# Rotary embedding: fp16 input resident from eight early loads, sums on TensorE, fp32 stores from SyncE

## Chip, cores and metric

The kernel runs on one core of one Trainium2 chip. The metric is the device time of one execution in microseconds, as the median over runs; lower is better.

## What is computed

The reference applies a rotary position embedding, with scaled positions, to x of shape 8 x 8 x 1024 x 64 (batch, heads, sequence, head size) in fp32. `scale` is 0.5.

```python
half = x.shape[-1] // 2
angles = np.outer(positions * scale, freqs)          # 1024 x 32
cos, sin = np.cos(angles), np.sin(angles)
out_first  = x[..., :half] * cos - x[..., half:] * sin
out_second = x[..., :half] * sin + x[..., half:] * cos
out = concatenate([out_first, out_second], axis=-1)  # fp32
```

The input and the output are 16.8 MB each. The cosine and sine depend on the position and the frequency, not on batch or head.

## The kernel before

The 64 (batch, head) pairs are taken as 16 units of four. In a unit, a partition holds 16 positions of a head: 64 partitions make one head, the 128 partitions hold two heads, and the free dimension holds two such pairs (`PU = 2`), 2 x 1024 elements. In DRAM each of these rows of 1024 elements is 4 KB of fp32.

Unit 0 is loaded as fp32 by SyncE (line 71). The positions (line 76, two transfers) and the frequencies (line 81) follow on the same queue. Units 1 to 15 are loaded by GpSimd's queue (line 90) with a cast to fp16 on the way, into seven rotating buffers; five are issued ahead of the loop, and each pass of the loop issues one more. GpSimd's queue also carries every store (line 153), which casts the fp16 result to fp32 on the way out, so loads and stores run through one queue in the order of issue.

The setup makes the tables: TensorE spreads the scaled frequencies over the partitions (line 86), VectorE forms the angles in turns (lines 97 to 116), 128 x 512, and ScalarE takes the sine four times (line 120), so that the table of the cosine and that of the sine each hold their 32 values twice in a row, for both halves of a head. They are fp16.

For each unit VectorE does four instructions: `pc`, the unit times the cosine (line 138), `ps`, the unit times the sine (line 139), each 128 x 2048, and the two half-width sums, a difference for the first halves (line 144) and a sum for the second (line 148), each 128 x 1024. The tile framework puts in the waits and orders the instructions of an engine by priority: in the trace the product `pc` of the next unit often stands ahead of the sums of the one before.

Of the kernel before, what the change touches and what calls it, by code (L numbers as in the profile page):

```python
# [1 line left out]

# [1 line left out]

# [4 lines left out]

FP32 = mybir.dt.float32
FP16 = mybir.dt.float16
AF = mybir.ActivationFunctionType
ALU = mybir.AluOpType

_MAGIC = 12582912.0
_TWO_PI_DN = float(np.float32(np.uint32(0x40C90FDA).view(np.float32)))

PAIRS_PER_UNIT = 2
PREFETCH = 5  # L20
BUF_X = 7
BUF_O = 7
BUF_P = 3


@with_exitstack
def kernel(
    ctx: ExitStack,
    tc: tile.TileContext,
    x: bass.AP,  # L30
    freqs: bass.AP,
    positions: bass.AP,
    scale: bass.AP,
    out: bass.AP,
):
    nc = tc.nc

    B, Hh, S, D = x.shape
    NBH = B * Hh
    half = D // 2  # L40
    P = nc.NUM_PARTITIONS
    HP = P // 2
    K = S // HP
    KD = K * D
    PU = PAIRS_PER_UNIT
    NU = NBH // (2 * PU)
    UKD = PU * KD
    assert S % HP == 0 and D == 2 * half and NBH % (2 * PU) == 0

    fscale = float(scale)  # L50

    xv = x.rearrange("b h s d -> (b h) (s d)")
    ov = out.rearrange("b h s d -> (b h) (s d)")

    def unit_dram(t, u):
        return t.rearrange("(i r) n -> i (r n)", r=2)[
            u * PU : (u + 1) * PU, :
        ].rearrange("i (p n) -> p i n", n=KD)

    consts = ctx.enter_context(tc.tile_pool(name="consts", bufs=1))  # L60
    tmp = ctx.enter_context(tc.tile_pool(name="tmp", bufs=2))
    psum = ctx.enter_context(tc.tile_pool(name="psum", bufs=1, space=bass.MemoryType.PSUM))
    xin0 = ctx.enter_context(tc.tile_pool(name="xin0", bufs=1))
    xin = ctx.enter_context(tc.tile_pool(name="xin", bufs=BUF_X))
    xout = ctx.enter_context(tc.tile_pool(name="xout", bufs=BUF_O))
    prods = ctx.enter_context(tc.tile_pool(name="prods", bufs=BUF_P))

    xtiles: dict[int, bass.AP] = {}

    X0 = xin0.tile([P, PU, KD], FP32)  # L70
    nc.sync.dma_start(out=X0, in_=unit_dram(xv, 0))  # L71
    xtiles[0] = X0

    pos_i64 = consts.tile([P, K], positions.dtype)
    for u in (0, 1):
        nc.sync.dma_start(  # L76
            out=pos_i64[u * HP : (u + 1) * HP, :],
            in_=positions.rearrange("(q k) -> q k", k=K),
        )
    freq_row = consts.tile([1, half], FP32)  # L80
    nc.sync.dma_start(out=freq_row, in_=freqs[None, :])

    coef = consts.tile([1, P], FP32)
    nc.vector.memset(coef, fscale / (2.0 * np.pi))  # L84
    cfreq = psum.tile([P, half], FP32)
    nc.tensor.matmul(out=cfreq, lhsT=coef, rhs=freq_row, start=True, stop=True)  # L86

    def load_unit(u):
        X = xin.tile([P, PU, KD], FP16, tag="X")
        nc.gpsimd.dma_start(out=X, in_=unit_dram(xv, u))  # L90
        xtiles[u] = X

    for u in range(1, min(1 + PREFETCH, NU)):
        load_unit(u)

    posf = consts.tile([P, K], FP32)
    nc.vector.tensor_copy(  # L97
        out=posf,
        in_=pos_i64.bitcast(mybir.dt.int32).rearrange("p (k t) -> p k t", t=2)[:, :, 0],
    )  # L100
    y = tmp.tile([P, K, half], FP32)
    nc.vector.tensor_tensor(  # L102
        out=y,
        in0=posf.unsqueeze(2).broadcast_to((P, K, half)),
        in1=cfreq.unsqueeze(1).broadcast_to((P, K, half)),
        op=ALU.mult,
    )
    yc = tmp.tile([P, K, half], FP32)
    nc.vector.tensor_scalar(out=yc, in0=y, scalar1=0.25, scalar2=None, op0=ALU.add)  # L109

    tabs = consts.tile([P, 2, K, D], FP16)
    for i, src in enumerate((yc, y)):
        m = tmp.tile([P, K, half], FP32, tag="m")
        nc.vector.tensor_scalar(out=m, in0=src, scalar1=_MAGIC, scalar2=None, op0=ALU.add)  # L114
        rneg = tmp.tile([P, K, half], FP32, tag="rneg")
        nc.vector.scalar_tensor_tensor(  # L116
            out=rneg, in0=m, scalar=_MAGIC, in1=src, op0=ALU.subtract, op1=ALU.subtract
        )
        for h in (0, 1):
            nc.scalar.activation(  # L120
                out=tabs[:, i, :, h * half : (h + 1) * half],
                in_=rneg,
                func=AF.Sin,
                bias=0.0,
                scale=-_TWO_PI_DN,
            )
    cosT = tabs[:, 0, :, :].rearrange("p k d -> p (k d)").unsqueeze(1).broadcast_to((P, PU, KD))
    sinT = tabs[:, 1, :, :].rearrange("p k d -> p (k d)").unsqueeze(1).broadcast_to((P, PU, KD))

    for u in range(NU):  # L130
        if u + 1 + PREFETCH < NU:
            load_unit(u + 1 + PREFETCH)
        X = xtiles.pop(u)
        OUT = xout.tile([P, PU, KD], FP16, tag="O")

        pc = prods.tile([P, PU, KD], FP16, tag="pc")
        ps = prods.tile([P, PU, KD], FP16, tag="ps")
        nc.vector.tensor_tensor(out=pc, in0=X, in1=cosT, op=ALU.mult)  # L138
        nc.vector.tensor_tensor(out=ps, in0=X, in1=sinT, op=ALU.mult)  # L139

        pcv = pc.rearrange("p i (k d) -> p (i k) d", d=D)
        psv = ps.rearrange("p i (k d) -> p (i k) d", d=D)
        ov_ = OUT.rearrange("p i (k d) -> p (i k) d", d=D)
        nc.vector.tensor_tensor(  # L144
            out=ov_[:, :, 0:half], in0=pcv[:, :, 0:half], in1=psv[:, :, half:D],
            op=ALU.subtract,
        )
        nc.vector.tensor_tensor(  # L148
            out=ov_[:, :, half:D], in0=psv[:, :, 0:half], in1=pcv[:, :, half:D],
            op=ALU.add,  # L150
        )

        nc.gpsimd.dma_start(out=unit_dram(ov, u), in_=OUT)  # L153


# [1 line left out]
_INS = ['x', 'freqs', 'positions', 'scale']  # L157
_OUTS = [((8, 8, 1024, 64), 'float32')]
#: Inputs that are plain numbers.
_NUMBERS = {'scale': 0.5}  # L160


# [26 lines left out]
```

## Time and profile before

| | |
|---|---|
| median of 4 runs | 87.27 us (86.94 to 87.54) |
| the profiled execution | 87.23 us |
| its span, first to last instruction | 85.3 us |
| VectorE busy | 61.4 us, 72 instructions |
| ScalarE busy | 3.5 us, 5 instructions |
| TensorE busy | 0.6 us, 2 instructions |
| GpSimd busy (it includes issuing transfers) | 22.6 us, 35 instructions |
| bytes read from and written to DRAM | 16.79 MB and 16.78 MB |
| transfers on GpSimd's queue | 8432 packets, 24.64 MB |
| transfers on SyncE's queue | 434 packets, 1.07 MB |

Busy times are sums over instructions that may overlap a little at their ends. Packet bytes are counted where they land, so a load that casts to fp16 counts half of what it reads. The difference of 1.93 us between the profiled execution and its span lies before the first and after the last instruction.

### The profile page before, as it was taken

How to read it: one execution, taken by the hardware profiler on the slowest of the kernel's cores; microseconds unless marked ns; L12 is line 12 of the kernel's file. 1: busy time of each engine (PE TensorE's matmuls, PEld its weight loads, DVE VectorE, ACT ScalarE, POOL GpSimd, SP SyncE). 2: the span in 40 equal slices, each digit the busy share in tenths (PEclk: the TensorE clock that was granted, in tenths of full speed). 3: DMA queues.
4: the chain of work that ended last, by engine and by line, in shares of the span. 5: the costliest groups of instructions: out<-in, count | busy, mean ns of one | idle time of the engine just before them, and what ended most of it. 6: DMA issues, size and time to landing. Idle time of an engine off the chain costs nothing.

```text
span 85.3 us, 193 instructions
## 1 busy us (share of the span) xinstructions
PE 0.6 (1%) x2; PEld 0.5 (1%) x2; DVE 61.4 (72%) x72; ACT 3.5 (4%) x5; POOL 22.6 (26%) x35
## 2 busy tenths in 40 slices
PE   0001000000000000000000000000000000000000
PEld 0001000000000000000000000000000000000000
DVE  0000879999999999999999999999998992000000
ACT  6000063000000000000000000000000000000000
POOL 4990000005215162460633612303213033000000
DMA  1899999999999999999999999999999999999970
GB/s 13 321 286 214 210 209 215 210 209 210 307 357 224 429 376 284 321 348 244 419 221 394 272 322 350 255 410 215 394 279 327 423 421 426 424 432 421 426 240 0
DMA packets 8867, 25.72 MB, mean 301 GB/s; under 512 B 674, under 2 KB 674, under 8 KB 8866
## 3 DMA queue, kind: packets, MB, share of 16 engines
q0 software_dynamic: 8432, 24.64, 107.3%
q1 hardware_dynamic: 434, 1.07, 3.7%
q14 instruction: 1, 0.01, 0.0%
HBM read 16.79 MB, written 16.78 MB: 394 GB/s over the span
## 4 chain that ended last, share of the span: by engine, by line
DVE 31%; DMA 22%; issue 20%; POOL 6%; SPq 2%; ACT 1%; POOLq 1%; PE 1%
DMA X<-in_x_dram 15%; DVE pc L138 11%; DVE ps L139 9%; DMA freq_row<-in_freqs_dram 6%; POOL out_dram L153 6%; DVE OUT L148 4%; DVE OUT L144 4%; ACT tabs L120 1%; SPq L76 1%; DVE m L114 1%; POOLq L184 1%; DVE y L102 1%; PE cfreq L86 1%; DVE rneg L116 1%; SPq L71 1%
## 5 line engine op out<-in xcount | busy, mean ns | idle before, releaser
L153 POOL DMA_DIRECT2D out_dram<-OUT x16 | 11.5, 720 | 47.8 <-DVE OUT L148 45.7
L138 DVE TENSOR_TENSOR pc<-X,tabs 128x2048 f16<-128x2048 f16 (+1 forms) x16 | 20.6, 1287 | 0.8 <-ACT tabs L120 0.6
L139 DVE TENSOR_TENSOR ps<-X,tabs 128x2048 f16<-128x2048 f16 (+1 forms) x16 | 20.6, 1287 | 0.0
L90 POOL DMA_DIRECT2D X<-in_x_dram x15 | 10.9, 727 | 1.2 <-POOLq L170 0.8
L144 DVE TENSOR_TENSOR OUT<-pc,ps 128x1024 f16<-128x1024 f16 x16 | 11.0, 687 | 0.0
L148 DVE TENSOR_TENSOR OUT<-ps,pc 128x1024 f16<-128x1024 f16 x16 | 11.0, 685 | 0.0
L97 DVE CAST posf<-pos_i 128x16 f32<-128x16 int32 x1 | 0.2, 175 | 7.1 <-DMA pos_i<-in_positions_dram 7.1
L120 ACT ACTIVATE tabs<-rneg 128x512 f16<-128x512 f32 x4 | 2.2, 618 | 9.3 <-DVE rneg L116 9.3
L120 ACT ACT_TABLE_LOAD x1 | 1.3, 1283 | 0.7 <-PEq L170 0.7
L102 DVE TENSOR_TENSOR y<-posf,cfreq 128x512 f32<-128x512 f32 x1 | 0.7, 689 | 0.6 <-PE cfreq L86 0.6
L84 DVE MEMSET coef<- 1x128 f32 x1 | 0.2, 165 | 0.8 <-PEq L170 0.8
L116 DVE SCALAR_TENSOR_TENSOR rneg<-m,y 128x512 f32<-128x512 f32 x1 | 0.7, 685 | 0.0
L116 DVE SCALAR_TENSOR_TENSOR rneg<-m,yc 128x512 f32<-128x512 f32 x1 | 0.7, 684 | 0.0
L86 PE MATMUL cfreq<-freq_row,coef 1*128 1x32 f32 x2 | 0.6, 391 | 8.1 <-DMA freq_row<-in_freqs_dram 8.1
L86 PEld LDWEIGHTS cfreq<-freq_row,coef 1*128 1x128 f32 x2 | 0.5, 308 | 8.1 <-issue 8.1
L109 DVE TENSOR_SCALAR yc<-y 128x512 f32<-128x512 f32 x1 | 0.4, 428 | 0.0
L114 DVE TENSOR_SCALAR m<-yc 128x512 f32<-128x512 f32 x1 | 0.4, 426 | 0.0
L114 DVE TENSOR_SCALAR m<-y 128x512 f32<-128x512 f32 x1 | 0.4, 419 | 0.0
L170 POOL MEMSET const-float32-0.0<- 128x1 f32 x1 | 0.1, 93 | 0.3 <-issue 0.3
L170 POOL MEMSET const-bfloat16-1.0<- 128x1 bf16 x1 | 0.1, 96 | 0.0
L170 POOL MEMSET const-float32-1.0<- 128x1 f32 x1 | 0.1, 93 | 0.0
L170 POOL MEMSET const-uint8-127<- 128x1 uint8 x1 | 0.1, 93 | 0.0
## 6 DMA issues: line engine op xcount, KB each, us to landing
out_dram<-OUT POOLq DMA_DIRECT2D x16, 1024.0 KB, 12.5
X<-in_x_dram POOLq DMA_DIRECT2D x15, 512.0 KB, 12.1
X<-in_x_dram SPq DMA_DIRECT2D x1, 1024.0 KB, 4.9
pos_i<-in_positions_dram SPq DMA_DIRECT2D x2, 8.0 KB, 5.3
freq_row<-in_freqs_dram SPq DMA_DIRECT2D x1, 0.1 KB
```

What stands on the lines that cost most here:

```text
L71: nc.sync.dma_start(out=X0, in_=unit_dram(xv, 0))
L86: nc.tensor.matmul(out=cfreq, lhsT=coef, rhs=freq_row, start=True, stop=True)
L90: nc.gpsimd.dma_start(out=X, in_=unit_dram(xv, u))
L102: nc.vector.tensor_tensor(out=y, in0=posf.unsqueeze(2).broadcast_to((P, K, half)), in1=cfreq.unsqueeze(1).broadcast_to((P, K, half)), op=A ...
L114: nc.vector.tensor_scalar(out=m, in0=src, scalar1=_MAGIC, scalar2=None, op0=ALU.add)
L116: nc.vector.scalar_tensor_tensor(out=rneg, in0=m, scalar=_MAGIC, in1=src, op0=ALU.subtract, op1=ALU.subtract)
L120: nc.scalar.activation(out=tabs[:, i, :, h * half : (h + 1) * half], in_=rneg, func=AF.Sin, bias=0.0, scale=-_TWO_PI_DN,)
L138: nc.vector.tensor_tensor(out=pc, in0=X, in1=cosT, op=ALU.mult)
L139: nc.vector.tensor_tensor(out=ps, in0=X, in1=sinT, op=ALU.mult)
L144: nc.vector.tensor_tensor(out=ov_[:, :, 0:half], in0=pcv[:, :, 0:half], in1=psv[:, :, half:D], op=ALU.subtract,)
L148: nc.vector.tensor_tensor(out=ov_[:, :, half:D], in0=psv[:, :, 0:half], in1=pcv[:, :, half:D], op=ALU.add,)
L153: nc.gpsimd.dma_start(out=unit_dram(ov, u), in_=OUT)
```

## The change

The layout, the queues and the place of the sums change.

- A unit is still four heads, but a partition holds 32 positions of one head: 32 partitions a head, one row of 2048 elements (8 KB of fp32) a partition. The position and angle tiles are therefore twice as wide, 128 x 1024 for the angles.
- All of x is resident: unit 0 as fp32 from SyncE, units 1 to 15 as fp16 by seven loads of 1, 1, 2, 2, 3, 3 and 3 units from GpSimd's queue, all issued ahead of the loop. No load waits for a buffer.
- Positions (four transfers) and frequencies are issued from ScalarE's queue.
- The cosine table holds its 32 values once and is read with a zero step for the two halves. The sine table holds minus sine for the first half and sine for the second.
- The two sums leave VectorE. GpSimd builds an fp16 identity; TensorE multiplies it with `pc` and then with `ps`, whose halves are read in swapped order, accumulating in PSUM: four pairs of 512-column matmuls a unit. The sign in the sine table turns the sum into the difference where it is wanted.
- ScalarE copies each 128 x 1024 of PSUM (two banks; three such buffers) to an fp32 output tile of 128 x 2048; there are six of these.
- SyncE stores the output tile without a cast.

```diff
-PAIRS_PER_UNIT = 2
-PREFETCH = 5
-BUF_X = 7
-BUF_O = 7
+GROUPS = (1, 1, 2, 2, 3, 3, 3)
+BUF_O = 6
 BUF_P = 3
+BANK = 512
...
-    HP = P // 2
+    HEADS = 4
+    HP = P // HEADS
     K = S // HP
-    KD = K * D
+    N = K * D
...
-    X0 = xin0.tile([P, PU, KD], FP32)
-    nc.sync.dma_start(out=X0, in_=unit_dram(xv, 0))
+    X0 = xin.tile([P, N], FP32, name="X0")
+    nc.sync.dma_start(out=X0, in_=xv[:, 0, :])
...
-    for u in (0, 1):
-        nc.sync.dma_start(
+    for h in range(HEADS):
+        nc.scalar.dma_start(
...
-    nc.sync.dma_start(out=freq_row, in_=freqs[None, :])
+    nc.scalar.dma_start(out=freq_row, in_=freqs[None, :])
+
+    u0 = 1
+    for g, n in enumerate(GROUPS):
+        X = xin.tile([P, n, N], FP16, name=f"X{g + 1}")
+        nc.gpsimd.dma_start(out=X, in_=xv[:, u0 : u0 + n, :])
+        for i in range(n):
+            xtiles[u0 + i] = X[:, i, :]
+        u0 += n
+
+    ident = consts.tile([P, P], FP16)
+    nc.gpsimd.memset(ident, 0.0)
+    nc.gpsimd.affine_select(
+        out=ident, in_=ident, compare_op=ALU.not_equal, fill=1.0, base=0,
+        pattern=[[-1, P]], channel_multiplier=1,
+    )
...
+    cosT = consts.tile([P, K, half], FP16)
+    sinT = consts.tile([P, K, 2, half], FP16)
...
+    nc.scalar.activation(out=cosT, in_=rc, func=AF.Sin, bias=0.0, scale=-_TWO_PI_DN)
+    rs = reduced(y, "s")
+    for h, sign in ((0, -1.0), (1, 1.0)):
+        nc.scalar.activation(
+            out=sinT[:, :, h, :], in_=rs, func=AF.Sin, bias=0.0, scale=sign * _TWO_PI_DN
+        )
+    cos_b = cosT.unsqueeze(2).broadcast_to((P, K, 2, half))
...
-        nc.vector.tensor_tensor(
-            out=ov_[:, :, 0:half], in0=pcv[:, :, 0:half], in1=psv[:, :, half:D],
-            op=ALU.subtract,
-        )
-        nc.vector.tensor_tensor(
-            out=ov_[:, :, half:D], in0=psv[:, :, 0:half], in1=pcv[:, :, half:D],
-            op=ALU.add,
-        )
-
-        nc.gpsimd.dma_start(out=unit_dram(ov, u), in_=OUT)
+        OUT = xout.tile([P, N], FP32, tag="O")
+        for b in range(N // BLK):
+            acc = psum.tile([P, KB, 2, half], FP32, tag="acc")
+            for c in range(BLK // BANK):
+                kk = BANK // D
+                kl = slice(c * kk, (c + 1) * kk)
+                kg = slice(b * KB + c * kk, b * KB + (c + 1) * kk)
+                nc.tensor.matmul(out=acc[:, kl, :, :], lhsT=ident, rhs=pc[:, kg, :, :], start=True, stop=False)
+                nc.tensor.matmul(out=acc[:, kl, :, :], lhsT=ident, rhs=ps[:, kg, ::-1, :], start=False, stop=True)
+            nc.scalar.copy(
+                out=OUT[:, b * BLK : (b + 1) * BLK], in_=acc.rearrange("p k h j -> p (k h j)")
+            )
+        nc.sync.dma_start(out=ov[:, u, :], in_=OUT)
```

The helper `reduced` holds the two VectorE instructions that before stood in the table loop (add and subtract a large constant, to take off whole turns); the multiplications `pc` and `ps` keep their form, with `cos_b` and `sinT` as tables.

More of the change, by code (lines that the diff above doesn't have):

```diff
@@ L12 @@
 FP16 = mybir.dt.float16
+I32 = mybir.dt.int32
 AF = mybir.ActivationFunctionType
@@ L41 @@
     P = nc.NUM_PARTITIONS
-    HP = P // 2
+    HEADS = 4
+    HP = P // HEADS
     K = S // HP
-    KD = K * D
[L45 to L48, printed above, removed]
-    fscale = float(scale)
[L52 to L58, printed above, removed]
+    N = K * D
+    NU = NBH // HEADS
+    BLK = 2 * BANK
+    KB = BLK // D
+    assert S % HP == 0 and D == 2 * half and NBH % HEADS == 0 and sum(GROUPS) == NU - 1
+    fscale = float(scale)
+    xv = x.rearrange("b h s d -> (b h s d)").rearrange("(u p n) -> p u n", p=P, n=N)
+    ov = out.rearrange("b h s d -> (b h s d)").rearrange("(u p n) -> p u n", p=P, n=N)
     consts = ctx.enter_context(tc.tile_pool(name="consts", bufs=1))
[L61 to L64, printed above, removed]
+    tmp = ctx.enter_context(tc.tile_pool(name="tmp", bufs=1))
+    setup_psum = ctx.enter_context(tc.tile_pool(name="setup_psum", bufs=1, space=bass.MemoryType.PSUM))
+    psum = ctx.enter_context(tc.tile_pool(name="psum", bufs=3, space=bass.MemoryType.PSUM))
+    xin = ctx.enter_context(tc.tile_pool(name="xin", bufs=1))
     xout = ctx.enter_context(tc.tile_pool(name="xout", bufs=BUF_O))
     prods = ctx.enter_context(tc.tile_pool(name="prods", bufs=BUF_P))
-    xtiles: dict[int, bass.AP] = {}
-    X0 = xin0.tile([P, PU, KD], FP32)
-    nc.sync.dma_start(out=X0, in_=unit_dram(xv, 0))
-    xtiles[0] = X0
+    X0 = xin.tile([P, N], FP32, name="X0")
+    nc.sync.dma_start(out=X0, in_=xv[:, 0, :])
+    xtiles = {0: X0}
     pos_i64 = consts.tile([P, K], positions.dtype)
-    for u in (0, 1):
-        nc.sync.dma_start(
-            out=pos_i64[u * HP : (u + 1) * HP, :],
+    for h in range(HEADS):
+        nc.scalar.dma_start(
+            out=pos_i64[h * HP : (h + 1) * HP, :],
             in_=positions.rearrange("(q k) -> q k", k=K),
@@ L80 @@
     freq_row = consts.tile([1, half], FP32)
-    nc.sync.dma_start(out=freq_row, in_=freqs[None, :])
+    nc.scalar.dma_start(out=freq_row, in_=freqs[None, :])
[12 more added lines that the diff above has]
+    )
     coef = consts.tile([1, P], FP32)
     nc.vector.memset(coef, fscale / (2.0 * np.pi))
-    cfreq = psum.tile([P, half], FP32)
+    cfreq = setup_psum.tile([P, half], FP32)
     nc.tensor.matmul(out=cfreq, lhsT=coef, rhs=freq_row, start=True, stop=True)
[L88 to L94, printed above, removed]
     posf = consts.tile([P, K], FP32)
@@ L98 @@
         out=posf,
-        in_=pos_i64.bitcast(mybir.dt.int32).rearrange("p (k t) -> p k t", t=2)[:, :, 0],
+        in_=pos_i64.bitcast(I32).rearrange("p (k t) -> p k t", t=2)[:, :, 0],
     )
@@ L107, with reduced @@
     )
[L108 to L113, printed above, removed]
+    cosT = consts.tile([P, K, half], FP16)
+    sinT = consts.tile([P, K, 2, half], FP16)
+    def reduced(src, tag):
+        m = tmp.tile([P, K, half], FP32, name="m" + tag)
         nc.vector.tensor_scalar(out=m, in0=src, scalar1=_MAGIC, scalar2=None, op0=ALU.add)
-        rneg = tmp.tile([P, K, half], FP32, tag="rneg")
+        rneg = tmp.tile([P, K, half], FP32, name="rneg" + tag)
         nc.vector.scalar_tensor_tensor(
@@ L118 @@
         )
[L119 to L125, printed above, removed]
-            )
[L127 to L144, printed above, removed]
-            out=ov_[:, :, 0:half], in0=pcv[:, :, 0:half], in1=psv[:, :, half:D],
-            op=ALU.subtract,
-        )
-        nc.vector.tensor_tensor(
-            out=ov_[:, :, half:D], in0=psv[:, :, 0:half], in1=pcv[:, :, half:D],
-            op=ALU.add,
-        )
-        nc.gpsimd.dma_start(out=unit_dram(ov, u), in_=OUT)
@@ new lines, in reduced @@
+        return rneg
+    yc = tmp.tile([P, K, half], FP32)
+    nc.vector.tensor_scalar(out=yc, in0=y, scalar1=0.25, scalar2=None, op0=ALU.add)
+    rc = reduced(yc, "c")
+    nc.scalar.activation(out=cosT, in_=rc, func=AF.Sin, bias=0.0, scale=-_TWO_PI_DN)
[5 more added lines that the diff above has]
+    cos_b = cosT.unsqueeze(2).broadcast_to((P, K, 2, half))
@@ new lines @@
+    for u in range(NU):
+        X = xtiles.pop(u).rearrange("p (k h j) -> p k h j", h=2, j=half)
+        pc = prods.tile([P, K, 2, half], FP16, tag="pc")
+        ps = prods.tile([P, K, 2, half], FP16, tag="ps")
+        nc.vector.tensor_tensor(out=pc, in0=X, in1=cos_b, op=ALU.mult)
+        nc.vector.tensor_tensor(out=ps, in0=X, in1=sinT, op=ALU.mult)
+        OUT = xout.tile([P, N], FP32, tag="O")
[9 more added lines that the diff above has]
+                out=OUT[:, b * BLK : (b + 1) * BLK], in_=acc.rearrange("p k h j -> p (k h j)")
+            )
+        nc.sync.dma_start(out=ov[:, u, :], in_=OUT)
```

## The prediction

> **What bounds the kernel now.** I read the page's slices first, then the stages by windows, then the groups, then the waits. Slices (section 2 of the page; each digit is the busy tenth of one fortieth of the span, 2.13 us):
>
> ```profile
> DVE  0000879999999999999999999999998992000000
> DMA  1899999999999999999999999999999999999970
> GB/s 13 321 286 214 210 209 215 210 209 210 307 357 224 429 376 284 321 348 244 419 221 394 272 322 350 255 410 215 394 279 327 423 421 426 424 432 421 426 240 0
> ```
>
> The DMA engines are full from the second slice to the last but one. VectorE looks full too, but from slice 11 on its 9s end 12 us before the transfers do. GB/s counts bytes at the destination, so a load that casts fp32 to fp16 shows half of what it reads: 210 there and 425 in the stores are the same pace. Windows put numbers on it (the last two columns are DMA share and GB/s):
>
> ```profile
> 2.00:4.00 2.00, 0.00 (x0) 0.00 (x0) 0.00 (x0) 0.03 (x1) 2.00 (x4) 1.00 0.73 289
> 6.00:18.00 12.00, 0.60 (x2) 0.50 (x2) 8.72 (x10) 2.19 (x4) 0.39 (x1) 1.00 1.13 211
> 22.00:64.00 42.00, 0.00 (x0) 0.00 (x0) 42.00 (x50) 0.00 (x0) 13.66 (x19) 1.00 1.19 322
> 66.00:82.00 16.00, 0.00 (x0) 0.00 (x0) 4.77 (x6) 0.00 (x0) 1.44 (x2) 1.00 1.25 425
> 82.00:84.00 2.00, 0.00 (x0) 0.00 (x0) 0.00 (x0) 0.00 (x0) 0.00 (x0) 1.00 0.16 49
> ```
>
> A unit is four (batch, head) rows, 1 MiB in fp32. A load lands 524,288 B at 211 GB/s: 2.485 us. A store lands 1,048,576 B at 425: 2.467 us. Sixteen of each, unit 0's plain load taken as a store: 15 x 2.485 + 17 x 2.467 = 79.2 us. The transfers run from about 2.1 to 82.4 us, 80.3 us, so about 1 us (the ramp at 289 GB/s) is all that is not full rate. The mixed stage 22:64 agrees: loads at 211 and stores at 425 that share 42 us and land 322 x 42 = 13.5 MB need 20.2 us of loads, 8.1 units; from 5 us (unit 0 landed) to 22 the queue did 17 / 2.485 = 6.8 of fifteen, so 8.2 were left. Alternating whole loads and whole stores costs nothing.
>
> The groups and waits say the same of the engines:
>
> ```profile
> L138 DVE TENSOR_TENSOR pc<-X,tabs 128x2048 f16<-128x2048 f16 (+1 forms) x16 | 20.6, 1287 | 0.8 <-ACT tabs L120 0.6
> L144 DVE TENSOR_TENSOR OUT<-pc,ps 128x1024 f16<-128x1024 f16 x16 | 11.0, 687 | 0.0
> L120 ACT ACTIVATE tabs<-rneg 128x512 f16<-128x512 f32 x4 | 2.2, 618 | 9.3 <-DVE rneg L116 9.3
> L102 DVE TENSOR_TENSOR y<-posf,cfreq 128x512 f32<-128x512 f32 x1 | 0.7, 689 | 0.6 <-PE cfreq L86 0.6
> ```
> ```profile
> 71.11 0.72 POOL L153 DMA_DIRECT2D out_dram<-OUT  x1 [1.75 <-DVE OUT L148]
> ```
>
> The last store is issued at 71.1 us and the transfers behind it run to 82.4: eleven microseconds of queue. The chain of waits names VectorE for a third of the span, but the kernel is **bound by its transfers**.
>
> **What the Trainium skill says.** "DMA: Bandwidth & Descriptors", section "Where 436 GB/s comes from": a ceiling of 435 GB/s for 16 engines; "Why small descriptors are slow": some three cycles (at 850 MHz, 3.5 ns) per packet. The trace agrees for stores: at 425 GB/s an engine needs 4,096 / (425 / 16) = 154.2 ns a row, at 435.2 it would be 150.6, so 3.6 ns over; for cast loads (422 at the source) 155.3, 4.7 over. Same page, "Queues, rings and completion order": an engine serves its queues in turn, packet by packet; the trace before has one queue carrying nearly everything, so it can't show who wins. "TensorE: Matmul & The Clock Gate", "Back-to-back issue gap": 512 columns take 427 ns with the clock gate cold, 216 warm, and "LDWEIGHTS" gives 107 ns for 128 columns; no row here shows either, and the gate is said to open after some 3.4 us of busy work. "VectorE: DVE Perf Modes", "What auto-detection actually checks": 16-bit operands with unit step run two elements a cycle; L144, on runs of 32, agrees: (1024 / 2) / 0.96 = 533 ns of its 687.
>
> **The change, part by part.**
>
> *Transfers.* The bytes at the larger side of each transfer stay: loads read fp32, stores write fp32. Rows grow from 4 KB to 8 KB, so if a row stays one packet an engine handles 8 packets a unit, not 16: 8 x 4.7 = 38 ns less for a load, 8 x 3.6 = 29 for a store, 16 x 67 = **1.07 us less**. If rows are cut at 4 KB: 0. Below nothing: fine mixing of two directions on one engine could cost; I allow 3% of the mixed stage (39 us, below), 1.1 us. I take the gain, because per-packet cost is what the rate shows.
>
> *Start.* Unit 0's load is SP's first issue as now; POOL's first load too. Five small issues (0.45 to 0.58 us each in SP's rows, 2.5 us) move to ScalarE's queue, maybe behind its 1.28 us table load; they no longer sit behind unit 0 on one ring. So positions and frequencies land at 6 to 11 us (now about 8); I take 8. Tables are 1024 wide: by L102 (one a cycle) y and the two rneg grow from 0.69 to 1.22, the three tensor_scalars (0.43, two a cycle) to 0.69. y, yc, m, rneg: 8.8 + 1.2 + 0.7 + 0.7 + 1.2 = 12.6 us; cosine by ScalarE 618 + 427 = 1.05; the sine's m and rneg hold VectorE to 14.5; pc and ps of the fp32 unit 0 (2.29 in the trace, 2.2 in steps) end at 18.9 (sines at 16.6); four matmuls 1.7, two copies 2.1: first store near **22.5 us, not 19.7**. Cost nothing: loads cover it, since all fifteen are queued early (seven issues of 0.7 us; if cost goes with rows, 7.5 x 0.72 = 5.4) and last alone to 2.1 + 16 x 2.45 = 41 us. POOL's identity comes behind these issues, at 7 to 9 us; first wanted at 18.9. Only if POOL had to wait for room in its ring would it be late, and then loads still fill the engines.
>
> *Compute per unit.* Removed: both half-width VectorE sums, 16 x (0.69 + 0.69) = 22 us busy, 1.2 us a unit in steps; VectorE's unit falls from 3.48 us (store to store in the timeline) to 2 x 1.14 = 2.28, off the path both times. Added: eight matmuls, 1.7 (warm) to 3.4 (cold), and at worst eight weight loads of 0.107 each exposed, 4.3; two ScalarE copies of 1024, 2 x 1.05 = 2.1. Sixteen stores move from POOL to SP, where each waits for the copy and nothing else is queued behind but the next store; ScalarE's copy waits for a free one of six OUT buffers, behind which matmuls wait through the three accumulators. That is back-pressure by transfers, the present bound.
>
> *Mixed stage.* At 22.5 us, (22.5 - 2.1) / 2.45 = 8.3 units have landed. With even turns the other 7.7 take 2 x 2.45 each, to 60 us; 7.7 stores are done. Then 8.3 stores remain, 20 us, **to about 81**. The last load carries units 13 to 15, so unit 13 is stored at the earliest at 60 + 1 + 2.3 + 3.4 + 2.1 = 69 us; stores 8 to 12 keep the engines busy until 73. Units 14 and 15 follow in steps of 3.4 at most, before their turns at 75.5 and 78. No idle time.
>
> *End.* 82.4 to 85.3 of closing and 87.23 - 85.30 outside the span stay. Sum: 87.23 - 1.07 = 86.16 us; the median of the runs is 0.04 above the profiled one: **86.2**.
>
> **The rivals.**
>
> 1. *Nothing gained* (rows cut at 4 KB, or mixing eats it): 87.2, between 86.8 and 87.8. For: no row of 8 KB is in the trace before.
>
> 2. *Slower: stores take more than their turn.* Then stores drain as fast as they are computed, loads are held back, and the last load, of three units, lands with no store in hand. Extreme: 16 loads and 13 stores are behind it, 2.1 + 29 x 2.45 = 73; then 1 + 2.3 + 1.7 + 1.1 + 1.0 = 7 us idle, then three stores: 88 instead of 81, so 93. At a share of 0.6 the idle time is about 3 us: 89. It decides where fewer than some 2.5 stores wait when the last load lands: 7.7 s / (1 - s) > 10.5, s above 0.57. For: with 8 KB store packets against cast packets cut smaller, s is 0.67. Against: with equal packets, 0.5.
>
> 3. *An engine becomes the bound.* Unit 15 must be ready by 78 us: 22.5 + 15 p gives p = 3.7 us. Cold TensorE with every weight load exposed, 4.3: 87 + 2.5, 8 us late, 94. VectorE at one element a cycle, 2 x 2.2 = 4.4 by the fp32 unit: 88.5, 96. Against: a TensorE that is the bound is busy throughout, so its gate should be warm; L144 keeps its rate on runs of 32 and L138 with a broadcast operand.
>
> 4. *Faster: directions overlap.* Finely mixed, an engine's reads of HBM and writes to HBM could run beside each other, which one queue in turn can't show. A tenth of 39 us: 82. Against: a cast load is paced by its source even where it writes half, so the engine looks bound by what it reads, and fp32 stores read as much as they write (before, half).
>
> **How the numbers follow.** The forecast 0.42 (85.6 to 86.8), nothing gained 0.20, stores first 0.22 (88 to 93), engine-bound 0.10 (89 to 96), overlap 0.06 (80 to 85). About 0.5%, 0.44 us, is what a measurement can tell from no change. Faster: 0.42 + 0.06 = 0.48. Same: 0.18 of the second case. Slower: 0.22 + 0.10 + 0.02 = 0.34. The range 84.8 to 92.3 leaves out most of the overlap and the far end of cases two and three, under 0.2; the forecast's own range is 85.6 to 86.8.
>
> **What would show it.** Right: DMA digits of 9 throughout, half the packets, 428 GB/s or more in the last stage, ScalarE's and TensorE's last work 5 us or more before the end, SP waiting on copies without idle transfers. Wrong: DMA slices below 9 near the end with a wait of VectorE for X (rival 2); TensorE or VectorE busy to the end (rival 3); packets of 4 KB (rival 1); mixed slices whose loads and stores add to more than 435 (rival 4).

## The result, and the profile after

The changed kernel takes 86.79 us (median of 37 runs, 86.38 to 87.08), the kernel before 87.24 in the same rounds: ratio 0.9939, 95% interval 0.9926 to 0.9953. That is 0.45 us faster where 1.0 was forecast. It lies inside the forecast's own range of 85.6 to 86.8, at its very edge, where the range of rival 1 (nothing gained) begins. The profiled execution took 86.85 us with a span of 85.1.

The slices of the page after (as before, 2.13 us each):

```profile
PE   0000200024999888970793508747477740000000
DVE  0000698699999999999199940006995000000000
ACT  0410006800499998822608035090987775000000
DMA  1899999999999999999999999999999999999960
GB/s 15 316 297 214 210 212 214 212 216 216 214 216 198 252 316 302 316 310 301 339 297 320 306 302 320 310 387 424 431 420 428 428 428 420 424 428 428 431 285 8
```

Transfers are still full from end to end, and no engine's 9s reach the last quarter. GB/s shows the two queues at work together: 210 to 216 are loads alone, 300 to 340 the mixed stage, 420 to 431 stores alone. The queues of the page (packets, MB, share):

```profile
q1 hardware_dynamic: 2448, 17.83, 50.8%
q0 software_dynamic: 2032, 7.86, 46.2%
q10 hardware_dynamic: 194, 0.03, 0.3%
q8 instruction: 1, 0.02, 0.1%
```

Half the packets: a row of 8 KB is one packet on either queue. The line q8 was not there before; it is small and will matter. Windows of the kernel after:

```profile
6.00:18.00 12.00, 0.60 (x2) 0.60 (x3) 7.87 (x9) 3.06 (x3) 0.63 (x3) 1.00 1.07 214
30.00:54.00 24.00, 15.16 (x53) 5.74 (x52) 17.62 (x16) 11.73 (x13) 0.00 (x0) 0.87 1.04 311
66.00:82.00 16.00, 2.57 (x11) 0.87 (x9) 0.00 (x0) 4.32 (x5) 0.00 (x0) 0.68 1.01 427
82.50:83.00 0.50, 0.00 (x0) 0.00 (x0) 0.00 (x0) 0.00 (x0) 0.00 (x0) 0.50 0.08 33
83.00:83.50 0.50, 0.00 (x0) 0.00 (x0) 0.00 (x0) 0.00 (x0) 0.00 (x0) 0.50 0.08 33
```

Loads run at 214 instead of 211, stores at 427 instead of 425. The last two rows are a tail: a DMA share of 0.06 is one engine of sixteen. The kernel before has nothing left after 83:

```profile
82.50:83.00 0.50, 0.00 (x0) 0.00 (x0) 0.00 (x0) 0.00 (x0) 0.00 (x0) 1.00 0.09 25
83.00:83.50 0.50, 0.00 (x0) 0.00 (x0) 0.00 (x0) 0.00 (x0) 0.00 (x0) 1.00 0.00 0
```

The costliest groups, the waits, and the closing line of each kernel (first L184 of the kernel before, then L187 of the one after; DRAIN and EVENT_SEMAPHORE are instructions with which each engine ends the program; columns: least, median and largest duration in ns, first and last start in us):

```profile
L153 ACT COPY OUT<-acc 128x1024 f32<-128x1024 f32 x32 | 30.7, 1019 | 24.0 <-DMA out_dram<-OUT 17.3
L151 PE MATMUL acc<-pc,ident 128*128 128x512 f16 x64 | 27.3, 427 | 21.9 <-ACT OUT L153 12.9
```
```profile
ACT OUT L153 <- DMA out_dram<-OUT: 17.3, 9, 3.4
```
```profile
L184 POOLq EVENT_SEMAPHORE  x4: 17/17/17, 84.6 to 85.2; - x4
L184 POOLq DRAIN  x3: 45/102/13467, 71.1 to 85.0; - x3
L184 SPq DRAIN  x3: 7/7/7, 83.6 to 84.8; - x3
```
```profile
L187 POOLq EVENT_SEMAPHORE  x4: 17/17/17, 84.3 to 85.0; - x4
L187 POOLq DRAIN  x3: 39/93/51937, 6.4 to 84.8; - x3
L187 SPq DRAIN  x3: 7/7/7, 84.2 to 85.0; - x3
```

ScalarE waits for stores to land before it can refill a tile, and the matmuls wait for ScalarE: back-pressure by transfers, as forecast. (The 427 ns of a matmul here are a mean of recorded durations, not the step from one to the next: at 25 us the profile records 0.38 us for one and the next begins after 0.215.) The closing is new to the argument. SyncE reaches its drain when all stores have landed, at 83.6 us before and at 84.2 after: **later by 0.6 us in the faster kernel**. Before, GpSimd is the last to come: its drain began at 71.1 and took 13.467 us, to 84.55, and the first closing semaphore follows at 84.6. After, GpSimd's drain ended at 58 and the semaphore follows SyncE at once.

A transfer ends with sixteen completion steps, one per DMA engine. With the last of them, as the trace has it, the profiled executions divide like this (us; "behind" is from the last step to the end of the span, "outside" is the rest of the time):

| kernel | last step | behind | outside | profiled time |
|---|---|---|---|---|
| before | 83.23 | 2.07 | 1.93 | 87.23 |
| after | 84.04 | 1.02 | 1.79 | 86.85 |

So the transfers ended 0.81 us later, and 1.05 + 0.14 us were won behind them. The second part is no chance of one execution: "outside" is 1.94 us in the mean of all later runs of the kernel before and 1.78 in the 37 of the changed one. The experiments ask for both.

### The profile page after: what moved, and what is told of

It reads as the page before. It is cut to its first block, busy times and chain, and to the rows that moved or that the text cites. A ratio compares the mean times of both kernels' runs of the same rounds, so it can differ in the third digit from the quotient of the medians.

```text
span 85.1 us, 475 instructions
## 1 busy us (share of the span) xinstructions
PE 36.0 (42%) x130; PEld 14.1 (17%) x130; DVE 44.6 (52%) x40; ACT 35.0 (41%) x36; POOL 5.6 (7%) x13
## 4 chain that ended last, share of the span: by engine, by line
DMA 50%; ACT 11%; DVE 10%; PE 6%; ACTq 3%; issue 2%; DVEq 0%
DMA out_dram<-OUT 44%; ACT OUT L153 10%; DMA freq_row<-in_freqs_dram 7%; PE acc L152 3%; DVE pc L141 3%; DVE ps L142 3%; PE acc L151 2%; ACTq L72 2%; DVE y L106 1%; DVE rnegc L120 1%; ACT cosT L128 1%; ACTq L187 1%; DVE yc L126 1%; PE cfreq L98 1%; DVE mc L118 1%
## 5 line engine op out<-in xcount | busy, mean ns | idle before, releaser
L153 ACT COPY OUT<-acc 128x1024 f32<-128x1024 f32 x32 | 30.7, 1019 | 24.0 <-DMA out_dram<-OUT 17.3
L151 PE MATMUL acc<-pc,ident 128*128 128x512 f16 x64 | 27.3, 427 | 21.9 <-ACT OUT L153 12.9
L152 PE MATMUL acc<-ps,ident 128*128 128x512 f16 x64 | 26.5, 428 | 2.6 <-DVE ps L142 2.6
L141 DVE TENSOR_TENSOR pc<-X,cosT 128x2048 f16<-128x2048 f16 (+1 forms) x16 | 20.6, 1288 | 11.6 <-PE acc L151 8.5
L142 DVE TENSOR_TENSOR ps<-X,sinT 128x2048 f16<-128x2048 f16 (+1 forms) x16 | 20.6, 1285 | 0.0
L152 PEld LDWEIGHTS <-ident 128*128 128x128 f16 x64 | 6.7, 105 | 33.0 <-issue 28.3
L151 PEld LDWEIGHTS <-ident 128*128 128x128 f16 x64 | 6.9, 107 | 13.0 <-issue 7.5
L131 ACT ACTIVATE sinT<-rnegs 128x1024 f16<-128x1024 f32 x2 | 2.1, 1048 | 9.0 <-DVE rnegs L120 9.0
L82 POOL DMA_DIRECT2D X<-in_x_dram x7 | 4.9, 729 | 0.8 <-POOLq L173 0.8
L106 DVE TENSOR_TENSOR y<-posf,cfreq 128x1024 f32<-128x1024 f32 x1 | 1.2, 1222 | 0.8 <-PE cfreq L98 0.8
L120 DVE SCALAR_TENSOR_TENSOR rnegs<-ms,y 128x1024 f32<-128x1024 f32 x1 | 1.2, 1219 | 0.0
L128 ACT ACTIVATE cosT<-rnegc 128x1024 f16<-128x1024 f32 x1 | 1.1, 1056 | 0.1
```

Source lines behind the costliest of these rows:

```text
L82: nc.gpsimd.dma_start(out=X, in_=xv[:, u0 : u0 + n, :])
L106: nc.vector.tensor_tensor(out=y, in0=posf.unsqueeze(2).broadcast_to((P, K, half)), in1=cfreq.unsqueeze(1).broadcast_to((P, K, half)), op=A ...
L120: nc.vector.scalar_tensor_tensor(out=rneg, in0=m, scalar=_MAGIC, in1=src, op0=ALU.subtract, op1=ALU.subtract)
L128: nc.scalar.activation(out=cosT, in_=rc, func=AF.Sin, bias=0.0, scale=-_TWO_PI_DN)
L131: nc.scalar.activation(out=sinT[:, :, h, :], in_=rs, func=AF.Sin, bias=0.0, scale=sign * _TWO_PI_DN)
L141: nc.vector.tensor_tensor(out=pc, in0=X, in1=cos_b, op=ALU.mult)
```

## The experiments

Theory A, formed after these profiles: the gain is in the closing, and inside the transfers three terms nearly cancel: fewer packets (less), mixing of directions and an instruction fetch (more). Theory B is the prediction's: fewer packets are all of it. All ratios below are to the kernel before; where a run is set against the changed kernel, its ratio is 0.9939. For each run, "last step" is the last completion step of its profile.

**1. Only the last store from GpSimd's queue.**

```diff
-        nc.sync.dma_start(out=ov[:, u, :], in_=OUT)
+        store = nc.gpsimd if u == NU - 1 else nc.sync
+        store.dma_start(out=ov[:, u, :], in_=OUT)
```

> The changed kernel, with only unit 15's store issued from GpSimd's queue instead of SyncE's. Theory A: about 0.9 us of the change's gain lies behind the last packet, because a GpSimd queue that still carries a store holds GpSimd's closing drain until some 1.3 us after that store has landed (in the kernel before the drain ends at 84.55 us, the last landing is at 83.23). So 0.7 to 1.2 us slower than the changed kernel: 87.6 to 87.9, as slow as the kernel before or slower. Theory B, that the gain is the halved number of packets as the prediction has it: no difference, 86.8.

Measured: 86.91 us, ratio 0.9948 (0.9927 to 0.997): as the changed kernel, so A's number failed. But the run didn't make the condition. Alone on its queue, unit 15's store took turns with units 13 and 14 on the other and was done by 81.2 us; GpSimd's drain ended at 81.9, ahead of SyncE's stores. It says nothing for or against the closing.

**2. All stores from GpSimd's queue.**

```diff
-        nc.sync.dma_start(out=ov[:, u, :], in_=OUT)
+        nc.gpsimd.dma_start(out=ov[:, u, :], in_=OUT)
```

> The changed kernel, with all sixteen stores issued from GpSimd's queue; one queue then does all loads first (to about 42 us) and all stores after. Theory A: the closing costs 0.9 us again, but the mixed stage at 421 GB/s instead of 428 (0.5 us) and the dip at the first stores (0.5 us) are gone: within 0.3 us of the changed kernel, 86.6 to 87.1. Theory B: queue and mixing cost nothing, so 86.8 too, with DMA's last landing where it was. The last landing tells them apart: A has it about 1 us earlier than in the changed kernel, B has it at the same time.

Measured: 87.72 us, ratio 1.0037 (1.0014 to 1.0059), slower than A had it, against B altogether. Its closing lines:

```profile
L187 POOLq EVENT_SEMAPHORE  x4: 17/17/17, 84.8 to 85.4; - x4
L187 POOLq DRAIN  x3: 40/93/13347, 71.4 to 85.2; - x3
```

The last step was at 83.72, 0.32 us ahead of the changed kernel with loads and stores apart (A had said about 1 us), but 1.75 us lay behind it, and 2.44 outside the span instead of 1.79. GpSimd's drain again ended 1.0 us after the last step. The stores' queue makes the closing longer: +0.73 behind and, in the mean of the 22 runs (2.32 against 1.78), +0.54 outside. Why the part outside is longer here than the 1.94 of the kernel before, which stores from the same queue, is not shown.

**3. Stores held until all loads have landed.**

```diff
+    hold = consts.tile([1, 64], FP16)
+    nc.sync.dma_start(out=hold, in_=xtiles[NU - 1][0:1, 0:64])
     for u in range(NU):
```

> The changed kernel, with a copy of 128 bytes out of unit 15's tile as SyncE's first instruction after unit 0's load: SyncE waits until the last load has landed (about 42 us), so that loads and stores are not mixed, and the stores still come from SyncE. Theory A: the dip and the loss of the mixed stage go, about 1.0 us: 85.8 (85.5 to 86.2). Theory B, mixing costs nothing: 86.8. A third outcome: TensorE and ScalarE, held until 42 us with six tiles full, can't keep the pace of 2.45 us a store after it, and idle transfers at the end make it slower than 87.5.

Measured: 88.5 us, ratio 1.014 (1.0104 to 1.0177). None of the three, though the last was nearest: the idle time is not at the end but between the loads and the first store.

```profile
GB/s 30 329 280 206 215 217 215 212 214 214 215 215 214 215 212 215 217 215 212 64 280 416 431 435 427 431 423 416 408 420 423 423 423 431 442 423 435 431 227 8
```

The 64 and the 280 are 2.3 us in which the small copy and then the first store start up. A hold needs loads still in the queue to cover it.

**4 and 7. The layout with 8 KB rows alone, in the kernel before.**

```diff
-PAIRS_PER_UNIT = 2
+PAIRS_PER_UNIT = 1
+HEADS = 4
...
-    HP = P // 2
+    HP = P // HEADS
```

> The kernel before, with one part of the change alone: the layout with 8 KB rows (a unit is 128 partitions of 2048 elements, tables twice as wide). Loads, sums on VectorE, casting stores from GpSimd and their order stay. Theory B: 16 x (35 + 17) ns by the rates of the changed kernel's pure stages (loads 214 against 211 GB/s, stores 428 against 425), or 1.07 us by the prediction: 86.2 to 86.4. Theory A agrees on the packets: 86.4. If it is 87.2, rows of 8 KB give nothing and the gain is from elsewhere. Tables start VectorE's loop 3 us later, which loads cover.

Measured: 89.42 us, ratio 1.0241 (1.0199 to 1.0283). The cover was not enough: with seven buffers the queue ran dry (36 in the row below, slice 11) while VectorE started 3 us later.

```profile
GB/s 30 337 274 210 214 214 210 214 217 219 36 360 268 275 435 380 197 408 247 375 296 311 352 260 395 240 405 249 369 300 315 423 435 420 427 438 427 427 161 0
```

So the early loads in the change are what pays for its longer setup. With `PREFETCH = 9` and `BUF_X = 11` the layout can be judged:

> The run with 8 KB rows in the kernel before (layout alone) again, with nine loads ahead instead of five and eleven load buffers instead of seven, so that loads cover the later start of VectorE and the transfers have no idle stretch at 22 us. By the pure stages' rates (35 ns a load and 17 ns a store unit) the last landing comes 0.8 us earlier than in the kernel before: 82.4 instead of 83.2, and 86.4 in time. If rows of 8 KB bring nothing at equal cover: 87.2. The closing with GpSimd's drain stays.

Measured: 86.9 us, ratio 0.9957 (0.9934 to 0.9979), last step at 82.83, 0.40 us ahead of the kernel before, with 2.07 behind it as there. **Fewer packets are worth 0.4 us**, not 1.07: a transfer has 8 fewer per DMA engine, so 0.40 us over 32 transfers is 1.6 ns a packet where 3.6 to 4.7 were taken. The deeper queue of loads was not tried without the layout; the DMA digits of the kernel before show no idle slice that it could fill. Stores of this run:

```profile
66.00:80.00 14.00, 0.00 (x0) 0.00 (x0) 8.29 (x11) 0.00 (x0) 1.59 (x3) 1.00 1.12 428
```

**5. Fewer TensorE instructions.** The sums of units 3 to 8 go to VectorE:

```diff
+        if u in VECTOR_UNITS:
+            ov_ = OUT.rearrange("p (k h j) -> p k h j", h=2, j=half)
+            for h in (0, 1):
+                nc.vector.tensor_tensor(
+                    out=ov_[:, :, h, :], in0=pc[:, :, h, :], in1=ps[:, :, 1 - h, :], op=ALU.add
+                )
+            nc.sync.dma_start(out=ov[:, u, :], in_=OUT)
+            continue
```

> The changed kernel, with the sums of units 3 to 8 made by VectorE (two half-width adds into the fp32 output tile) instead of TensorE and ScalarE; stores stay on SyncE. TensorE's program shrinks from about 260 to 164 instructions. Theory A (new after the first runs): at 55 us one 16 KB packet on an instruction queue takes 947 ns of one DMA engine; from then to the end one of the sixteen completion steps of each store comes 1.1 us after the others, so the last store lands 1.1 us late. It is TensorE's program that is fetched. Without the fetch, 0.8 to 1.1 us less: 85.7 to 86.0, and no 16 KB packet in the trace. If the fetch is another engine's, the packet and 86.8 stay. Theory B (packets alone): 86.8. VectorE gets 6 x 2.3 us more, which its idle time in the mixed stage covers.

Measured: 86.09 us, ratio 0.9875 (0.9849 to 0.9901), 0.7 us under the changed kernel by the medians (4 runs here) and 0.6 by the ratios, just above what A gave. q8 is gone from the page, and with it the tail of one engine:

```profile
82.50:83.00 0.50, 0.00 (x0) 0.00 (x0) 0.00 (x0) 0.00 (x0) 0.00 (x0) 0.50 0.05 16
83.00:83.50 0.50, 0.00 (x0) 0.00 (x0) 0.00 (x0) 0.00 (x0) 0.00 (x0) 0.50 0.00 0
```

The last step came at 83.38 instead of 84.04, and the closing stayed at 1.02.

**6. More TensorE instructions.** 160 matmuls of 64 columns that nobody reads, in TensorE's idle time:

```diff
+    idle_matmuls(64)
     for u in range(NU):
+        if 3 <= u <= 10:
+            idle_matmuls(12)
```

> The changed kernel with 160 more matmuls of 64 columns into a spare PSUM tile that nobody reads (64 ahead of the loop, 12 in each of units 3 to 10), to double the suspected cost. Theory A: [...]one or two more packets of 16 KB; on the same DMA engine the last landing moves out by 0.95 us each, 87.7 to 88.7; on another engine it stays at 86.8 to 87.0. Theory B: 86.8, since TensorE has idle time for them in the mixed stage.

Measured: 86.94 us, ratio 0.9972 (0.9958 to 0.9985).

```profile
q8 instruction: 2, 0.03, 0.1%
```
```profile
82.50:83.00 0.50, 0.00 (x0) 0.00 (x0) 0.00 (x0) 0.00 (x0) 0.00 (x0) 0.50 0.12 49
83.00:83.50 0.50, 0.00 (x0) 0.00 (x0) 0.00 (x0) 0.00 (x0) 0.00 (x0) 0.50 0.15 66
```

Two fetches, 921 and 960 ns, and now two engines in the tail (0.12 and 0.15): the last two of the sixteen steps come at 83.97 and 83.98, the others by 83.14. The second fetch fell to another engine, so the end of this execution hardly moved; over all runs the time is 0.15 us longer by the medians and 0.3 by the ratios. That is A's second branch.

**8. Stores cut into two of 4 KB rows.**

```diff
-            nc.scalar.copy(
-                out=OUT[:, b * BLK : (b + 1) * BLK], in_=acc.rearrange("p k h j -> p (k h j)")
-            )
-        nc.sync.dma_start(out=ov[:, u, :], in_=OUT)
+            blk = slice(b * BLK, (b + 1) * BLK)
+            nc.scalar.copy(out=OUT[:, blk], in_=acc.rearrange("p k h j -> p (k h j)"))
+            nc.sync.dma_start(out=ov[:, u, blk], in_=OUT[:, blk])
```

> The changed kernel with each unit's store cut into two of 4 KB rows (one after each ScalarE copy), loads as they are: undoes 8 KB rows for the stores alone. By the pure stages, 17 ns a unit x 16 = 0.3 us slower, by the prediction 29 x 16 = 0.5: 87.0 to 87.3. Turns: if engines change queue after each packet, a 4 KB store packet against an 8 KB load packet gives loads two thirds of the mixed stage, so the last load lands near 46 us instead of 58.

Measured: 87.45 us, ratio 1.0002 (0.998 to 1.0024): slower than the changed kernel by 0.66 us in the medians and 0.55 in the ratios, more than both expectations. Twice as many transfers go with the shorter rows here; the run does not separate the two.

```profile
30.00:48.00 18.00, 10.27 (x38) 3.85 (x36) 14.30 (x14) 7.71 (x8) 0.00 (x0) 0.81 1.06 275
54.00:80.00 26.00, 13.42 (x51) 5.17 (x49) 9.26 (x8) 13.54 (x14) 0.00 (x0) 0.76 1.03 419
```

Uncast 4 KB packets store at 419 GB/s, below the casting ones of the kernel before (425). In the mixed stage the two queues start equal numbers of packets (138 loads to 137 stores in 28 to 32 us), though a load packet reads twice what a store packet moves (322 against 172 ns); so 275 GB/s, and the last load lands at 51 us, not at 57 as in the changed kernel (46 was too early). The counts are even from the first microsecond on: **the engines change queue after each packet**, as far as a trace that does not name the engine of a packet can show it.

**9. The last five stores of the kernel before from SyncE**, uncast, from fp32 tiles:

```diff
-        OUT = xout.tile([P, PU, KD], FP16, tag="O")
+        plain = u >= SP_FROM
+        pool, dt, tag = (tailout, FP32, "OF") if plain else (xout, FP16, "O")
+        OUT = pool.tile([P, PU, KD], dt, tag=tag)
...
-        nc.gpsimd.dma_start(out=unit_dram(ov, u), in_=OUT)
+        store = nc.sync if plain else nc.gpsimd
+        store.dma_start(out=unit_dram(ov, u), in_=OUT)
```

> The kernel before, with the last five units' sums written to fp32 tiles and stored by SyncE without a cast; loads and the first eleven stores stay on GpSimd's queue, rows stay 4 KB. GpSimd's queue is then empty some time before the end. Theory A (closing): in all kernels so far the span ends 1.0 to 1.1 us after the last landing where SyncE's stores land last (1.02, 1.08, 0.96, 1.02, 1.01, 1.02) and 1.75 to 2.07 where GpSimd's do. So the closing falls from 2.07 to 1.0, and the time by about 1.0 us, to 86.2, if the last landing stays near 83.2 (plain 4 KB packets cost some 2 ns more than casting ones, 5 x 16 x 2 = 0.2 us). Theory B, that the issuing queue doesn't matter and only packets do: 87.2 to 87.4. VectorE's fp32 sums add 5 x 1.1 us, so its last sum comes near 76 us, still before the queue is empty.

Measured: 86.97 us, ratio 0.9969 (0.9944 to 0.9994): the sign is A's, a third of the size. Its closing lines:

```profile
L189 POOLq EVENT_SEMAPHORE  x4: 17/17/17, 84.1 to 84.7; - x4
L189 POOLq DRAIN  x3: 39/108/25132, 54.2 to 84.6; - x3
L189 SPq DRAIN  x3: 7/7/7, 84.0 to 84.3; - x3
```

GpSimd's drain ended at 79.3 us, and only 1.33 us lay behind the last step instead of 2.07. The last step moved out to 83.52, in line with uncast 4 KB packets and mixing. 0.74 us won behind it, 0.29 lost in the transfers. The 0.31 us that are left to the changed kernel's 1.02 are SyncE's: it still goes through eight short waits after the last step, 61 ns apart, and reaches its drain 0.52 us after it, where the changed kernel has three and 0.21. The profiled execution (86.62) is one of the fastest of this run; in the mean of all runs "outside" is 1.79, as in the changed kernel, and in the median one the span is only 0.15 us shorter than before.

**10. TensorE instructions alone, in the kernel before:** 160 idle matmuls, 320 instructions.

```diff
+    for _ in range(160):
+        nc.tensor.matmul(out=junk, lhsT=ident, rhs=tabs[:, 0, 0, :], start=True, stop=True)
```

> The kernel before with 160 matmuls of 64 columns on idle TensorE (they read the tables and an all-ones tile, and write a PSUM tile that nobody reads): 320 more TensorE instructions and nothing else. Theory A: one or two 16 KB packets on an instruction queue, each 0.95 us of one DMA engine; the last landing comes 0.6 to 1.0 us later, 87.8 to 88.2. Theory B: TensorE is idle and not on the path: 87.2.

Measured: 87.7 us against 87.28, ratio 1.0057 (1.0033 to 1.008). One q8 packet of 962 ns at 20 us; the last step at 83.86, the one before it at 82.96. TensorE was idle otherwise: **the added instructions alone cost 0.4 to 0.6 us.** The median came out 0.1 us under A's lower number. In its profile:

```profile
q8 instruction: 1, 0.02, 0.1%
```
```profile
83.00:83.50 0.50, 0.00 (x0) 0.00 (x0) 0.00 (x0) 0.00 (x0) 0.00 (x0) 0.50 0.05 16
```

**11. Both cures: run 5, and the stores held by the sixth load** (units 10 to 12), with 5 us or more of loads still queued:

```diff
+    hold = consts.tile([1, 64], FP16)
+    nc.sync.dma_start(out=hold, in_=xtiles[sum(GROUPS[:-1])][0:1, 0:64])
     for u in range(NU):
```

> The run with six units' sums on VectorE, and SyncE's stores held by a 128-byte copy out of the sixth load's tile (units 10 to 12), so that the mixed stage begins near 36 us instead of 28 while 5 us of loads are still queued and no transfer time is lost. Theory A: a third of the mixed stage (421 against 428 GB/s) goes, 0.2 us; the dip at the first stores stays: 85.9, hard to tell from 86.1. If the hold leaves the engines without work it is slower than 86.5.

Measured: **85.52 us, ratio 0.9797 (0.9766 to 0.9828)**, 0.57 us better than run 5 where 0.2 had been expected (6 runs here, 4 there).

```profile
24.00:38.00 14.00, 3.80 (x14) 1.33 (x12) 14.00 (x13) 4.03 (x5) 0.00 (x0) 0.80 1.06 214
38.00:46.00 8.00, 0.00 (x0) 0.00 (x0) 3.50 (x4) 0.00 (x0) 0.00 (x0) 0.50 1.04 292
46.00:80.00 34.00, 15.70 (x56) 5.91 (x56) 26.20 (x23) 13.58 (x14) 0.00 (x0) 0.75 1.01 427
```

The last step comes at 82.76. The middle of the mixed stage of run 5, for comparison:

```profile
30.00:54.00 24.00, 1.03 (x2) 0.28 (x3) 24.00 (x22) 0.00 (x0) 0.00 (x0) 0.54 1.04 312
```

There packets of both directions ran side by side from 28.3 to 56.7 us, here from 40.2 to 45.3: the stores were issued from 36.3 us on, as planned, but their first packet came four microseconds later. So four fifths of the mixed stage went, not a third. Taking each packet at the pure rates (214 and 427 GB/s), run 5 lost 1.0 us between 26 and 58 us, 0.6 of it before 30, at the start of the stores; this run lost 0.5 between 38 and 46, most of it again at the start. The difference of 0.5 us is most of the 0.62 between the last steps.

## Why the prediction was right, and where not

*The bound* was right: transfers are full before and after, and everything forecast to be hidden was hidden. Nearly even turns, one packet a row, ScalarE and TensorE far from the path, VectorE at 1.13 us a product in steps with a broadcast table (1.14 forecast): all as written. The first store was issued at 24.5 us, not 22.5 (VectorE and ScalarE took the sine ahead of the cosine, and first matmuls ran at 430 ns), and loads covered it. Rivals 2 and 3 (stores first; an engine as the bound) have nothing for them, nor has rival 4: counted at the larger side, the mixed stage moved 421 GB/s, less than the pure stages. TensorE's steps fell from 0.43 to 0.215 us at 24 us, 3.7 us after its steady work began. The Trainium skill's "TensorE: Matmul & The Clock Gate", section "Back-to-back issue gap", gives these two values, 427 and 216 ns. One price had no line behind it, the 427 ns for 512 more columns on ScalarE; the trace has 438 (1056 against 618 ns).

*The size* came from a sum with one term, -1.07. The runs show four (us, last steps and closings of profiled executions):

| term | forecast | measured | by |
|---|---|---|---|
| packets of 8 KB | -1.07 | -0.40 | run 7 against before |
| mixed stage and its start | 0 (bound +1.1) | +0.63, at least | run 11 against run 5 |
| instruction fetch | not seen | +0.66 | run 5 against after |
| closing, behind and outside | "stay" | -1.19 | table above; runs 2 and 9 |

They add to -0.30, where the profiled executions differ by 0.38 and the medians by 0.45. Inside the transfers rival 1 came nearer than the forecast: mixing and the fetch ate more than the packets gave. **Right in sign and range, then, by luck: the gain that was forecast was used up, and one of about the same size came from a place that was taken as fixed.** The forecast's own sign, 428 GB/s or more in the last stage, came out at 427. The steps that failed:

- "I take the gain" on packets. Price and place were mine from a ceiling of the Trainium skill ("DMA: Bandwidth & Descriptors", "Where 436 GB/s comes from": 435 GB/s; the pure stages here come to 428 at most) and the rates before; the loads did go from 211 to 214 (2.485 to 2.450 us), but the stores only from 425 to 427. It fits that an uncast packet is dearer than a casting one: 419 against 425 at 4 KB (run 8 and before), 427 against 428 at 8 KB (after and run 7), and uncast stores from GpSimd's queue run at 427 too (run 2). What the pure stages give, 16 x (35 + 12) ns = 0.75, is more than run 7's 0.40. Part of this is one late engine in run 7's profile, late since 57 us, when an instruction packet of 342 ns ran: the last step stands 0.34 us behind the fifteenth, against 0.15 before, and the fifteenth steps are 0.59 apart. The rest is open.
- Mixing. The packets of the changed kernel's trace tell what it cost. In 30 to 54 us 641 load packets and 592 store packets started; at 214 and 427 GB/s they need 12.3 + 11.4 us, so 0.4 of 24 us went, 1.5%. In 26 to 30 us, around the first store, 139 and 44 need 2.7 + 0.8 us, so 0.5 of 4 us went. With 0.1 at the end it is 1.0 us, near the 1.1 that was allowed for, but half of it comes at the start and not from the mixing that the 3% meant. (The stage that the prediction worked out, 22.5 to 60 us, is 37.5 us long, not 39.) Taking one end of a stated bound as the value was the choice that failed. Why packets of two directions take longer side by side is not shown; that it needs two queues is not either, as run 2 mixed nothing.
- "*End.* 82.4 to 85.3 of closing and 87.23 - 85.30 outside the span stay." The row of GpSimd's 13.5 us drain was in the trace before. I had read the end of the transfers and the end of the span and called the 2.9 us between them fixed. Runs 2 and 9 each show some 0.7 of the 1.05 us won behind the last step, and run 9 what the other 0.3 are; what happens outside the span is open.
- The program's length. Its 128 matmuls and as many weight loads were counted for their time on TensorE, not for being fetched through the same DMA engines that were the bound.

## What to carry to other kernels

When transfers are the bound, count everything that uses a DMA engine, instruction fetches too, and look at the last step of the slowest engine rather than at mean GB/s. Ask which queue's stores are the last to land: here GpSimd's kept its closing drain open for 1.0 to 1.3 us after them. Loads may be queued early and stores started late, as long as enough loads are still queued to cover the first store's start, some 4 us here.

## What the runs showed of the hardware

- A long TensorE program is fetched in packets of 16 KB, 921 to 965 ns each, by one DMA engine per packet: none with 82 matmuls, one with 130 or 162, two with 290. One of the sixteen completion steps of every later transfer then comes 0.8 to 1.2 us after the others (two of them in run 6).
- The span ended 0.95 to 1.1 us after the last step where GpSimd's queue had long been empty, 1.33 in run 9, and 1.75 to 2.07 where its stores were last.
- A store queued behind long loads on another queue waits: issued at 24.46 us, its first packet started at 28.1 (3.4 us after the issue in run 8, 3.9 in run 11, but 1.1 in run 3, where no load was queued), and from then the turns were nearly even. Around that start (26 to 28 us) loads alone fell to 174 GB/s.
- GpSimd's seven load issues took 0.56 to 0.70 us with 128 rows and 0.78 to 0.80 with 384, three times as many.
